# A hybrid Conformer/Mamba-2 block on one core: the order in which DVE issues the norm's multiplications and ACT the gate's sigmoids

## The chip, the core and the metric

The kernel runs on one core of a Trainium2 chip. A core has a matrix engine (TensorE, PE), a vector engine (VectorE, DVE), a scalar engine (ScalarE, ACT), a general engine (GpSimd, POOL) and a queue that starts transfers (SyncE, SP). Each works through its own list of instructions in order; semaphores make one wait for another. The metric is the device time of one launch in microseconds (us), the median of several runs.

## The reference

One layer over 1024 positions and 1024 channels in float32:

```python
u = h @ w_in[l]
u_glu, z, xbc, dt_raw, gate_a, gate_b = split_in(u)
y_a = conformer_branch(u_glu, ...)   # GLU, 31-tap depthwise conv, layer norm, SiLU, @ w_conv_out
y_b = ssd_branch(z, xbc, dt_raw, ...)
mix = (jax.nn.sigmoid(gate_a) * y_a + jax.nn.sigmoid(gate_b) * y_b) @ w_o[l]
h = layer_norm(DN_ALPHA * h + mix, ...)
ffn = conv_ffn(h, ...)
h = layer_norm(DN_ALPHA * h + ffn, ...)
```

The SSD branch ends, group by group (four groups of 512 channels), in a gated norm whose statistic is taken over the group's channels for each position:

```python
yg = (y * jax.nn.silu(z)).reshape(bsz, t, SSM_GROUPS, SSM_DIM // SSM_GROUPS)
yg = yg * lax.rsqrt(jnp.mean(jnp.square(yg), axis=-1, keepdims=True) + RMS_EPS)
yn = yg.reshape(bsz, t, SSM_DIM) * norm_w
return yn @ w_out
```

## The kernel before

Channels lie on the 128 partitions and positions run along the free axis. The 1024 positions are worked through in two halves of 512 (`hh` 0 and 1). Each half runs through `mixers`, `combine` and an output product; the FFN follows.

**Products.** Float32 accuracy comes from a split of both operands into a high and a low part, so that one step of a product is three matmuls (L170, L171, L172: high by high, high by low, low by high; only the third reads the low part of the weights). One product of `project` is eight such steps, 24 matmuls, into one of four PSUM banks of the pool `acc`. `weights` (L142) brings a 128x1024 block for each product: SyncE loads it (`st`, three buffers), ACT casts the high part (L147) and DVE subtracts for the low part (L151), into `w` (three buffers). In half 1 the low parts of most blocks are read back from memory instead.

**Mixers.** For each group g, PE makes the products for B, C and x, the gate z and two columns of the Conformer branch. DVE does the 4-tap convolutions (L408) and, as a filler of low priority, the 31-tap convolution, one tap of 128x512 an instruction (L453, c<-v). `ssd_group` then runs four chunks of 128 positions: ACT makes the decay matrix `m` (L504, L511), DVE multiplies it (L531), PE forms the chunk's output from it (L536, L539), and DVE adds the skip term to that output (L554, four instructions), gates it (L562) and, with ACT's squares (L564), sums up `ssum` (L565, L566). At the next group `scaled` turns `ssum` into the norm's row: PE sums over partitions (L573), ACT takes the root (L581), DVE the reciprocal (L582), POOL stores the row (L584) and loads it again spread over all partitions as `rstd` (L585), and DVE multiplies the group's four tiles by it (L588, 128x512 each). `parts` splits the product into `yT` (L601 on ACT, L602 on DVE), which the products with `w_ssm_out` read.

**Combine.** PE makes gate products (weights `w_gb_0` to `w_gb_7`) and SSD output products (`w_sp_0` to `w_sp_7`) in turn: gb_0, gb_1, sp_0, gb_2, sp_1, gb_3, sp_2 and so on. A sigmoid on ACT (L721) empties a gate's bank into `gb`. DVE adds an earlier half of the SSD output, loaded as `yb` (L730), into `mb` (L735) and multiplies it by `gb` (L736). POOL adds the convolution's channels (L681, L683) for its layer norm.

**What sets the order.** The kernel is written in the order of the algorithm; a scheduler with a model of time and with priorities decides the order in which each engine issues its instructions. Weights have a high priority (offset 4000), the 31-tap convolution a low one (−1500).

Of the kernel before, what the change touches and what calls it, by code (L numbers as in the profile page):

```python
# [8 lines left out]
F32 = mybir.dt.float32  # L9
F32R = mybir.dt.float32r  # L10
AF = mybir.ActivationFunctionType
ALU = mybir.AluOpType
# [43 lines left out]
def kernel(  # L56
# [42 lines left out]
    later = statep.tile([P, P], F32, name="later")  # L99
# [39 lines left out]
    }  # L139
    y_scr = [dram.tile([8, P, HALF], F32, name=f"y_scr{i}") for i in range(2)]  # L140

    def weights(src, name, keep=None, kept=None):  # L142
        with tc.high_priority(offset=4000):
            st = wst.tile([P, D], F32, tag="st", name=f"st_{name}")
            SY.dma_start(st, src)
            w = wsp.tile([P, 2, D], F32R, tag="w", name=f"w_{name}")
            A.copy(w[:, 0, :], st)  # L147
            if kept is not None:
                SY.dma_start(w[:, 1, :].bitcast(F32), kept)
            else:  # L150
                V.tensor_tensor(  # L151
                    out=w[:, 1, :], in0=st, in1=w[:, 0, :].bitcast(F32), op=ALU.subtract
                )
            if keep is not None:
                SY.dma_start(keep, w[:, 1, :].bitcast(F32))
        return w

    def col_weights(hh, ct):
        scr = low_scr.get(ct)
        return weights(  # L160
            wcol[ct], f"c{hh}_{ct}", None if hh else scr, scr if hh else None
        )

    def big_tile(name):
# [301 lines left out]
    def z_gate(pl, hh, hT, g):  # L466
# [3 lines left out]
            A.activation(out=zs[:, i, :], in_=column(hh, hT, CT_Z + 4 * g + i), func=AF.Silu)  # L470
        return zs

    def ssd_group(pl, hh, g, xT, BT, CT, zs):
        S = states[g]
        h8 = slice(8 * g, 8 * g + 8)
# [8 lines left out]
        for c in range(4):  # L484
            nm = f"{hh}_{g}_{c}"
            cs = slice(c * P, (c + 1) * P)
            first = hh == 0 and c == 0
            last = hh == 1 and c == 3
            ab = pl.tile([P, 8, P], F32, tag="ab", name=f"ab{nm}")
            r = c * HEADS + 8 * g  # L490
            SY.dma_start(
                ab.rearrange("p h l -> p (h l)"),
                acs_scr[hh][r : r + 8, :].rearrange("h l -> (h l)").partition_broadcast(P),
            )
            px = bank(0)
            for i in range(4):
                TE.transpose(px[:, i * P : (i + 1) * P], xT[:, i, cs], ident)
            pb = bank(0)
            if not last:
                TE.transpose(pb[:, :P], BT[:, cs], ident)  # L500
            TE.matmul(pb[:, P : 2 * P], BT[:, cs], CT[:, cs], start=True, stop=True)
            m = pl.tile([P, 8, P], F32, tag="m", name=f"m{nm}")
            for h in range(8):
                A.activation(  # L504
                    out=m[:, h, :],
                    in_=ab[:, h, :],
                    func=AF.Relu,
                    scale=-1.0,
                    bias=acs[:, c, 8 * g + h : 8 * g + h + 1],
                )  # L510
            A.activation(out=m, in_=m, func=AF.Exp, scale=-1.0)  # L511
            if not first:
                ce = pl.tile([P, 8, P], F32, tag="ce", name=f"ce{nm}")
                A.activation(out=ce, in_=ab, func=AF.Exp)  # L514
                G.tensor_tensor(  # L515
                    out=ce, in0=ce, in1=CT[:, cs].unsqueeze(1).to_broadcast([P, 8, P]), op=ALU.mult
                )
            cbm = pl.tile([P, P], F32, tag="cbm", name=f"cbm{nm}")
            V.tensor_mul(cbm, pb[:, P : 2 * P], upper)
            xs = pl.tile([P, HALF], F32, tag="xs", name=f"xs{nm}")  # L520
            V.tensor_tensor(
                out=heads(xs), in0=heads(px), in1=per_head(dts[0][:, c, h8]), op=ALU.mult
            )
            if not last:
                xsd = pl.tile([P, HALF], F32, tag="xsd", name=f"xsd{nm}")
                V.tensor_tensor(
                    out=heads(xsd), in0=heads(px), in1=per_head(dts[1][:, c, h8]), op=ALU.mult
                )
                bt = pl.tile([P, P], F32, tag="bt", name=f"bt{nm}")
                A.copy(bt, pb[:, :P])  # L530
            V.tensor_tensor(out=m, in0=m, in1=cbm.unsqueeze(1).to_broadcast([P, 8, P]), op=ALU.mult)  # L531
            py = bank(0)
            for i in range(4):
                pair = [(2 * i + k, py[k * HP : (k + 1) * HP, i * P : (i + 1) * P]) for k in (0, 1)]
                for h, o in pair:
                    TE.matmul(o, xs[:, h * HP : (h + 1) * HP], m[:, h, :], start=True, stop=first)  # L536
                if not first:
                    for h, o in pair:
                        TE.matmul(  # L539
                            o, S[:, h * HP : (h + 1) * HP], ce[:, h, :], start=False, stop=True  # L540
                        )
            if not last:
                pn = bank(0)
                TE.matmul(pn, bt, xsd, start=True, stop=True)
                if first:
                    V.tensor_copy(S, pn)
                else:
                    V.tensor_tensor(
                        out=heads(S), in0=heads(S), in1=per_head(edc[:, 1, c, h8]), op=ALU.mult
                    )  # L550
                    V.tensor_add(S, S, pn)
            for i in range(4):
                k = PC_SD + 4 * g + i
                V.scalar_tensor_tensor(  # L554
                    out=xT[:, i, cs],
                    in0=xT[:, i, cs],
                    scalar=pc[:, k : k + 1],
                    in1=py[:, i * P : (i + 1) * P],
                    op0=ALU.mult,
                    op1=ALU.add,  # L560
                )
            V.tensor_mul(xT[:, :, cs], xT[:, :, cs], zs[:, :, cs])  # L562
            sq = pl.tile([P, 4, P], F32, tag="sq", name=f"sq{nm}")
            A.activation(out=sq, in_=xT[:, :, cs], func=AF.Square)  # L564
            V.tensor_add(sq[:, 0:2], sq[:, 0:2], sq[:, 2:4])  # L565
            V.tensor_add(ssum[:, cs], sq[:, 0], sq[:, 1])  # L566

        def scaled():
            rstd = pl.tile([P, HALF], F32, tag="rstd", name=f"rstd{hh}_{g}")
            rows = pl.tile([P, P], F32, tag="rows", name=f"rows{hh}_{g}")  # L570
            pv = bank(0)
            for j in range(4):
                TE.matmul(  # L573
                    pv[j * HEADS : (j + 1) * HEADS, :P],
                    ones[:, :HEADS],
                    ssum[:, j * P : (j + 1) * P],
                    start=True,
                    stop=True,
                    tile_position=(0, j * HEADS),
                )  # L580
            A.activation(out=rows, in_=pv[:, :P], func=AF.Sqrt, bias=eps, scale=1.0 / HALF)  # L581
            V.reciprocal(out=rows, in_=rows)  # L582
            scr = nrm_scr[hh * GROUPS + g]
            G.dma_start(scr, rows.rearrange("(j r) l -> j r l", j=4)[:, 0, :])  # L584
            G.dma_start(rstd, scr.rearrange("j l -> (j l)").partition_broadcast(P))  # L585
            for i in range(4):
                k = PC_NW + 4 * g + i
                V.scalar_tensor_tensor(  # L588
                    out=xT[:, i, :],
                    in0=xT[:, i, :],  # L590
                    scalar=pc[:, k : k + 1],
                    in1=rstd,
                    op0=ALU.mult,
                    op1=ALU.mult,
                )

        def parts(yT):
            ks = slice((g % 2) * 4, (g % 2) * 4 + 4)
# [60 lines left out]
    def combine(hh, hT, yT, accs):  # L659

        with pool(f"comb{hh}") as pl:
            gbs = []
            squares = pl.tile([P, 2, HALF], F32, tag="sq", name=f"csq{hh}")
            stats = pl.tile([P, 2, HALF], F32, tag="stats", name=f"stats{hh}")
            late, cs = [], []
# [50 lines left out]
            def gate():  # L716
                j = len(gbs)
                pg = bank(1)
                project(pg, weights(wcol[CT_GB + j], f"gb{hh}_{j}"), hT)
                gb = pl.tile([P, HALF], F32, tag="gate", bufs=3, name=f"gb{hh}_{j}")  # L720
                A.activation(out=gb, in_=pg, func=AF.Sigmoid)  # L721
                gbs.append(gb)

            gate()
            mb = None
            for j in range(8):
                if j < 7:
# [4 lines left out]
                    mb = early_tiles()  # L732
                ps = bank(1)
                project(ps, weights(wssm[j, 1], f"sp{hh}_{j}"), yT)
                V.tensor_add(mb[j], ya, ps)  # L735
                V.tensor_mul(mb[j], mb[j], gbs[j])  # L736
                if j == 2 - hh:
# [567 lines left out]
```

## Time and profile before

| | |
|---|---|
| median of 3 runs | 1966.11 us (1964.66 to 1969.19) |
| profiled execution | 1962.23 us |
| its span | 1960.5 us |
| granted TensorE clock | 0.998 |
| instructions in the span | 25846 |

The profile is of one execution. A line of a timeline gives start and duration (us), engine, program line, operation, the tiles out<-in, and in brackets how long the engine stood still before it and what ended that. A line of waits gives the total, the number and the longest of the waits of one group. Half 0's combine begins at 484 us (PE's first matmul with `w_gb_0`), half 1's at 1127 us.

### The profile page before, as it was taken

Reading aid. Unit: us, or ns where it says so; the run is one execution under the profiler, and the core shown is the slowest. Engines: PE = TensorE matmul, PEld = TensorE weight load, DVE = VectorE, ACT = ScalarE, POOL = GpSimd, SP = SyncE. Lnnn points to the kernel's source line nnn. Section 1 sums busy time; section 2 is a strip of 40 time slices with the busy share of each in tenths; the row PEclk is TensorE's granted clock in tenths of the full one; section 3 lists DMA queues with packets and bytes.
Section 4 is the critical chain, followed back from the end, with each engine's and each line's share of the span. In section 5 each row is a group of like instructions: output and inputs, shape, how many; then the busy total and the mean of one; then the engine's idle time right before and its main releaser. Section 6 shows DMA issues by size and latency. Waiting matters only on the chain.

```text
span 1960.5 us, 25846 instructions
## 1 busy us (share of the span) xinstructions
PE 1928.3 (98%) x9453; PEld 1572.2 (80%) x9453; DVE 1599.4 (82%) x2224; ACT 1083.5 (55%) x1617; POOL 216.8 (11%) x258
## 2 busy tenths in 40 slices
PE   9999999999999999999999999999999999989997
PEld 7888777777788788888778888888888888868886
DVE  7599999999887548898999646587788888879778
ACT  4666667654263266868775435365555555544432
POOL 0001000111310000110201130001000000121010
PEclk9999999999999999999999999999999999999999
DMA  7645455556446665555554744566445455588673
GB/s 265 223 167 209 162 193 183 172 167 220 142 168 205 211 218 183 191 185 196 190 173 155 233 139 129 176 248 225 167 171 185 165 198 173 184 299 296 196 227 130
DMA packets 127648, 378.36 MB, mean 193 GB/s; under 512 B 15104, under 2 KB 15648, under 8 KB 127520
## 3 DMA queue, kind: packets, MB, share of 16 engines
q1 hardware_dynamic: 107424, 318.48, 48.2%
q0 software_dynamic: 13760, 46.69, 6.9%
q10 hardware_dynamic: 6336, 11.54, 1.6%
q8 instruction: 74, 1.21, 0.2%
q14 instruction: 54, 0.44, 0.1%
HBM read 289.99 MB, written 86.65 MB: 192 GB/s over the span
## 4 chain that ended last, share of the span: by engine, by line
PE 57%; DVE 10%; DMA 5%; ACT 2%; issue 2%; SPq 0%; DVEq 0%; ACTq 0%
PE acc L172 13%; PE acc L171 13%; PE acc L170 13%; PE sm L171 5%; PE sm L172 5%; PE sm L170 5%; DVE c L453 3%; DMA dr<-wdown 1%; DMA dr<-b_scr 1%; DVE w_dn L1093 1%; DMA b_scr<-fo 1%; DVE x L408 1%; PE sm L536 1%; DVE rows L231 1%; DVE rows L234 1%
## 5 line engine op out<-in xcount | busy, mean ns | idle before, releaser
L170 PE MATMUL acc<-hT,w_c 128*128 128x512 f32 x1000 | 391.9, 392 | 0.6 <-ACT x L406 0.6
L172 PE MATMUL acc<-hT,w_c 128*128 128x512 f32 x1000 | 390.2, 391 | 0.6 <-DVE w_c L151 0.5
L171 PE MATMUL acc<-hT,w_c 128*128 128x512 f32 x1000 | 390.6, 391 | 0.0
L453 DVE SCALAR_TENSOR_TENSOR c<-v,pc,c 128x512 f32<-128x512 f32 x480 | 372.2, 801 | 7.1 <-ACT c L442 4.6
L170 PEld LDWEIGHTS acc<-hT,w_c 128*128 128x128 f32 x1000 | 187.8, 188 | 41.6 <-issue 1.9
L172 PEld LDWEIGHTS acc<-hT,w_c 128*128 128x128 f32 x1000 | 187.7, 188 | 41.4 <-DVE w_c L151 1.7
L171 PEld LDWEIGHTS acc<-hT,w_c 128*128 128x128 f32 x1000 | 187.8, 188 | 39.5 <-issue 1.1
L147 ACT CAST w_c<-st_c 128x1024 fp32r<-128x1024 f32 x128 | 133.8, 1045 | 108.9 <-PE acc L172 82.3
L515 POOL TENSOR_TENSOR ce<-ce,xbc 128x1024 f32<-128x1024 f32 x28 | 80.1, 2861 | 678.6 <-ACT ce L514 678.6
L1092 ACT CAST w_dn<-dr 128x1024 fp32r<-128x1024 f32 (+1 forms) x73 | 68.8, 945 | 86.4 <-DMA dr<-wdown 32.8
L504 ACT ACTIVATE m<-ab,acs 128x128 f32<-128x128 f32 x256 | 78.4, 390 | 48.9 <-PE sm L536 47.7
L170 PE MATMUL sm<-h1s,w_s 128*128 128x512 f32 x264 | 102.7, 389 | 0.0
L171 PE MATMUL sm<-h1s,w_s 128*128 128x512 f32 x264 | 102.7, 389 | 0.0
L172 PE MATMUL sm<-h1s,w_s 128*128 128x512 f32 x264 | 102.2, 389 | 0.0
L151 DVE TENSOR_TENSOR w_c<-st_c,w_c 128x1024 fp32r<-128x1024 f32 x64 | 79.0, 1237 | 22.3 <-ACT w_c L147 22.1
L408 DVE SCALAR_TENSOR_TENSOR x<-u,pc,x 128x512 f32<-128x512 f32 x96 | 79.7, 842 | 4.0 <-ACT x L406 3.8
L1093 DVE TENSOR_TENSOR w_dn<-dr,w_dn 128x1024 fp32r<-128x1024 f32 (+1 forms) x73 | 78.6, 1086 | 4.0 <-ACT w_dn L1092 4.0
L172 PE MATMUL acc<-h1b,w_ue 128*128 128x512 f32 x176 | 68.8, 394 | 0.2 <-DVE w_ue L151 0.2
L170 PE MATMUL acc<-h1b,w_ue 128*128 128x512 f32 x176 | 68.6, 390 | 0.0
L171 PE MATMUL acc<-h1b,w_ue 128*128 128x512 f32 x176 | 68.5, 389 | 0.0
L170 PE MATMUL sm<-h1b,w_s 128*128 128x512 f32 x176 | 68.5, 389 | 0.0
L171 PE MATMUL sm<-h1b,w_s 128*128 128x512 f32 x176 | 68.5, 389 | 0.0
(325 smaller groups left out, 4533.9 us busy)
## 6 DMA issues: line engine op xcount, KB each, us to landing
st_c<-wcol SPq DMA_DIRECT2D x128, 512.0 KB, 4.4
low_scr<-w_c SPq DMA_DIRECT2D x64, 512.0 KB, 2.9
w_c<-low_scr SPq DMA_DIRECT2D x64, 512.0 KB, 4.4
ab<-acs_scr SPq DMA_DIRECT2D x32, 512.0 KB, 4.1
dr<-wdown SPq DMA_DIRECT2D x55, 256.0 KB, 5.3
st_wo<-wo SPq DMA_DIRECT2D x24, 512.0 KB, 4.1
st_ue<-wup SPq DMA_DIRECT2D x22, 512.0 KB, 3.9
first_scr<-first ACTq DMA_DIRECT2D x44, 256.0 KB, 3.0
```

The lines of the kernel that those rows point to most:

```text
L147: A.copy(w[:, 0, :], st)
L151: V.tensor_tensor(out=w[:, 1, :], in0=st, in1=w[:, 0, :].bitcast(F32), op=ALU.subtract)
L170: TE.matmul(ps, wa(0), xa(0), start=start, stop=False, skip_group_check=more)
L171: TE.matmul(ps, wa(0), xa(1), start=False, stop=False, skip_group_check=more)
L172: TE.matmul(ps, wa(1), xa(0), start=False, stop=stop, skip_group_check=more)
L231: V.scalar_tensor_tensor(out=t, in0=t, scalar=mv[:, i, 0:1], in1=g, op0=ALU.subtract, op1=ALU.mult)
L408: V.scalar_tensor_tensor(out=o, in0=u[:, k : k + HALF], scalar=pc[:, wc + k : wc + k + 1], in1=o, op0=ALU.mult, op1=ALU.add,)
L453: V.scalar_tensor_tensor(out=accs[i], in0=v[:, k : k + HALF], scalar=pc[:, wc + k : wc + k + 1], in1=accs[i], op0=ALU.mult, op1=ALU.add,)
L504: A.activation(out=m[:, h, :], in_=ab[:, h, :], func=AF.Relu, scale=-1.0, bias=acs[:, c, 8 * g + h : 8 * g + h + 1],)
L515: G.tensor_tensor(out=ce, in0=ce, in1=CT[:, cs].unsqueeze(1).to_broadcast([P, 8, P]), op=ALU.mult)
L1092: A.copy(w[:, 0, cs], src)
L1093: V.tensor_tensor(out=w[:, 1, cs], in0=src, in1=w[:, 0, cs].bitcast(F32), op=ALU.subtract)
```

## The change

`weights` keeps a list of the casts and of the low parts that it issues. A new helper, `issue_after`, tells the scheduler to issue one instruction after another one of the same engine; it adds an order and no semaphore.

- The four multiplications by the norm's row (`held`) of groups 0 to 2 are to be issued after the last of the four skip additions (L554) of the next group's chunk 0. Those of group 3 are to be issued after the low part of `w_gb_0`, the first weights of `combine`.
- Each gate's sigmoid is to be issued ahead of the fifth cast of weights after its own: ahead of `w_gb_3`'s cast for gb_0.

```diff
+    casts, los = [], []
...
-            A.copy(w[:, 0, :], st)
+            casts.append(A.copy(w[:, 0, :], st))
...
+                los.append(
+                    V.tensor_tensor(
+                        out=w[:, 1, :], in0=st, in1=w[:, 0, :].bitcast(F32), op=ALU.subtract
+                    )
                 )
...
+    def issue_after(later, earlier):
+
+        tc.add_manual_dep(
+            later.ins,
+            earlier.ins.name,
+            mybir.DependencyInfo(mybir.DependencyClass.NoSync, mybir.DependencyReason.DATA),
+            reason="issue order",
+        )
...
+    held = []
...
-                V.scalar_tensor_tensor(
+                skip = V.scalar_tensor_tensor(
                     out=xT[:, i, cs],
...
+            while held and c == 0:
+                issue_after(held.pop(), skip)
...
-                V.scalar_tensor_tensor(
+                by_row = V.scalar_tensor_tensor(
                     out=xT[:, i, :],
...
+                held.append(by_row)
...
-                A.activation(out=gb, in_=pg, func=AF.Sigmoid)
+                sigmoids.append((len(casts), A.activation(out=gb, in_=pg, func=AF.Sigmoid)))
                 gbs.append(gb)
 
             gate()
+            while held:
+                issue_after(held.pop(), los[-1])
...
                 project(ps, weights(wssm[j, 1], f"sp{hh}_{j}"), yT)
+                for n, sigmoid in sigmoids:
+                    if len(casts) > n + 4:
+                        issue_after(casts[n + 4], sigmoid)
+                sigmoids = [(n, i) for n, i in sigmoids if len(casts) <= n + 4]
```

The added lines shift the numbers: L151, L453, L554, L588, L602, L721 and L735 of before are L154, L466, L569, L605, L620, L739 and L759 after. What the scheduler then makes of it is seen in each engine's order of instructions.

DVE in half 0, group 1, from the tap ahead of the multiplications of group 0 (`x_0_0`) to the skip additions of group 1's chunk 0 (`x_0_1`) and the work on chunk 1 (`xs_1_1`). Before:

```order
L453 SCALAR_TENSOR_TENSOR c_1_1347<-v_1_1102,pc,c_1_1347 128x512
L588 SCALAR_TENSOR_TENSOR x_0_0_713<-x_0_0_713,pc,rstd_0_1919 128x512 x4
L408 SCALAR_TENSOR_TENSOR xbc_18_2274<-u_18_2273,pc,xbc_18_2274 128x512
L453 SCALAR_TENSOR_TENSOR c_2_2176<-v_2_1845,pc,c_2_2176 128x512
L151 TENSOR_TENSOR w_c_26_2408<-st_c_26_2406,w_c_26_2408 128x1024
L554 SCALAR_TENSOR_TENSOR x_0_1_1493<-x_0_1_1493,pc,sm_1969 128x128 x4
L408 SCALAR_TENSOR_TENSOR xbc_22_2315<-u_22_2314,pc,xbc_22_2315 128x512
L546 COPY state_106<-sm_1978 128x512
L521 TENSOR_TENSOR xs_1_1_2015<-sm_1992,dtv 128x512
```

And after:

```order
L466 SCALAR_TENSOR_TENSOR c_1_1347<-v_1_1102,pc,c_1_1347 128x512
L421 SCALAR_TENSOR_TENSOR xbc_18_2274<-u_18_2273,pc,xbc_18_2274 128x512
L466 SCALAR_TENSOR_TENSOR c_2_2176<-v_2_1845,pc,c_2_2176 128x512
L154 TENSOR_TENSOR w_c_26_2408<-st_c_26_2406,w_c_26_2408 128x1024
L421 SCALAR_TENSOR_TENSOR xbc_18_2274<-u_18_2273,pc,xbc_18_2274 128x512
L569 SCALAR_TENSOR_TENSOR x_0_1_1493<-x_0_1_1493,pc,sm_1969 128x128 x4
L605 SCALAR_TENSOR_TENSOR x_0_0_713<-x_0_0_713,pc,rstd_0_1919 128x512 x4
L421 SCALAR_TENSOR_TENSOR xbc_22_2315<-u_22_2314,pc,xbc_22_2315 128x512
L466 SCALAR_TENSOR_TENSOR c_2_2176<-v_2_1845,pc,c_2_2176 128x512
L561 COPY state_106<-sm_1978 128x512
L536 TENSOR_TENSOR xs_1_1_2015<-sm_1992,dtv 128x512
```

The multiplications moved from ahead of the skip additions to right behind them, and one more instruction of the 4-tap convolution stands ahead of both.

DVE in half 0's combine, from the low parts of `w_sp_1` on. Before:

```order
L151 TENSOR_TENSOR w_sp_1_4622<-st_sp_1_4620,w_sp_1_4622 128x1024
L453 SCALAR_TENSOR_TENSOR c_6_4222<-v_6_3506,pc,c_6_4222 128x512
L453 SCALAR_TENSOR_TENSOR c_7_4224<-v_7_3574,pc,c_7_4224 128x512 x3
L151 TENSOR_TENSOR w_gb_3_4654<-st_gb_3_4652,w_gb_3_4654 128x1024
L453 SCALAR_TENSOR_TENSOR c_7_4224<-v_7_3574,pc,c_7_4224 128x512 x5
L151 TENSOR_TENSOR w_sp_2_4688<-st_sp_2_4686,w_sp_2_4688 128x1024
L453 SCALAR_TENSOR_TENSOR c_7_4224<-v_7_3574,pc,c_7_4224 128x512 x2
L735 TENSOR_TENSOR mb_0_4528<-yb_0_4526,acc_4553 128x512
```

And after:

```order
L154 TENSOR_TENSOR w_sp_1_4622<-st_sp_1_4620,w_sp_1_4622 128x1024
L466 SCALAR_TENSOR_TENSOR c_6_4222<-v_6_3506,pc,c_6_4222 128x512
L466 SCALAR_TENSOR_TENSOR c_7_4224<-v_7_3574,pc,c_7_4224 128x512 x10
L154 TENSOR_TENSOR w_gb_3_4654<-st_gb_3_4652,w_gb_3_4654 128x1024
L759 TENSOR_TENSOR mb_0_4528<-yb_0_4526,acc_4553 128x512
L154 TENSOR_TENSOR w_sp_2_4688<-st_sp_2_4686,w_sp_2_4688 128x1024
L760 TENSOR_TENSOR mb_0_4528<-mb_0_4528,gb_0_4492 128x512
```

All the taps that are left stand ahead of `w_gb_3`'s low parts now, eleven where four stood, and the addition to `mb_0` stands ahead of `w_sp_2`'s low parts. Further up in the same list, `w_gb_0`'s low parts now stand two taps later than the last tap ahead of the multiplications before, and the multiplications right behind them. From the multiplications of group 3 to `w_gb_3`'s low parts there are 28 taps, where there were 23; from the second low part of `yT` on, 24, where there were 20.

ACT in half 0's combine, from the cast of `w_sp_1` on. Before:

```order
L147 CAST w_sp_1_4622<-st_sp_1_4620 128x1024
L147 CAST w_gb_3_4654<-st_gb_3_4652 128x1024
L147 CAST w_sp_2_4688<-st_sp_2_4686 128x1024
L721 ACTIVATE gb_0_4492<-acc_4462 128x512
L721 ACTIVATE gb_1_4524<-acc_4494 128x512
L721 ACTIVATE gb_2_4615<-acc_4585 128x512
```

And after:

```order
L149 CAST w_sp_1_4622<-st_sp_1_4620 128x1024
L739 ACTIVATE gb_0_4492<-acc_4462 128x512
L149 CAST w_gb_3_4654<-st_gb_3_4652 128x1024
L739 ACTIVATE gb_1_4524<-acc_4494 128x512
L149 CAST w_sp_2_4688<-st_sp_2_4686 128x1024
L739 ACTIVATE gb_2_4615<-acc_4585 128x512
```

The three sigmoids, which stood together behind the cast of `w_sp_2`, now stand one by one among the casts.

Elsewhere the lists shift with these: on SyncE the load of `yb_0` stands behind the load for `w_gb_4` and no longer behind those for `w_sp_3` and `w_gb_5`; on PE the chunks' outputs of half 0 stand up to three matmuls later, and in half 1 those of chunks 1 to 3 stand 6 to 9 matmuls later in groups 1 and 2 and 15 in group 3; POOL's order is as it was.

More of the change, by code (lines that the diff above doesn't have):

```diff
@@ L150, in weights @@
             else:
-                V.tensor_tensor(
-                    out=w[:, 1, :], in0=st, in1=w[:, 0, :].bitcast(F32), op=ALU.subtract
+                los.append(
+                    V.tensor_tensor(
+                        out=w[:, 1, :], in0=st, in1=w[:, 0, :].bitcast(F32), op=ALU.subtract
+                    )
                 )
@@ L661, in combine @@
         with pool(f"comb{hh}") as pl:
-            gbs = []
+            gbs, sigmoids = [], []
             squares = pl.tile([P, 2, HALF], F32, tag="sq", name=f"csq{hh}")
```

## The prediction

> **What bounds the kernel now.** I read the page's busy shares, then TensorE's (PE's) waits, then VectorE's (DVE's) waits, then the two places where they meet. The busy shares:
>
> ```profile
> PE 1928.3 (98%) x9453; PEld 1572.2 (80%) x9453; DVE 1599.4 (82%) x2224; ACT 1083.5 (55%) x1617; POOL 216.8 (11%) x258
> ```
>
> PE is idle for 1960.5 − 1928.3 = 32 us of its span, and no order of DVE or ACT can win more than that and the slow restarts behind it. What the change can touch are waits of PE on DVE and ACT inside the two halves' mixers and combines. From the waits of PE over the whole span (total us, times, longest us):
>
> ```profile
> PE sm L536 <- DVE m L531: 3.3, 3, 1.4
> PE acc L172 <- DVE w_gb L151: 1.8, 2, 1.4
> PE acc L170 <- ACT gb L721: 1.6, 1, 1.6
> PE acc L172 <- DVE w_sp L151: 0.9, 1, 0.9
> PE acc L170 <- ACT x L406: 0.6, 1, 0.6
> PE acc L172 <- DVE w_c L151: 0.5, 1, 0.5
> ```
>
> They sum to 8.7 us in nine stalls. One stall costs a little more than its idle time, as PE's timeline at the first gate product of half 0 shows (start, duration):
>
> ```profile
> 484.20 0.39 PE L170 MATMUL acc<-hT,w_gb 128*128 128x512 f32 x1
> 484.43 0.39 PE L171 MATMUL acc<-hT,w_gb 128*128 128x512 f32 x1
> 486.23 0.50 PE L172 MATMUL acc<-hT,w_gb 128*128 128x512 f32 x1 [1.41 <-DVE w_gb L151]
> 486.57 0.40 PE L170 MATMUL acc<-hT,w_gb 128*128 128x512 f32 x1
> ...
> 517.37 0.39 PE L172 MATMUL acc<-hT,w_gb 128*128 128x512 f32 x1
> ```
>
> The steady pitch is 0.23. Here 1.80 passes, 1.57 too much, and the next start is 0.11 late too: 1.68 for 1.41 of idle time, 0.27 more. So the nine stalls are worth 8.7 + 9 × 0.27 = 11.1 us: the ceiling of this change. By place: the mixers of half 0 hold m once (1.4), x (0.6) and w_c (0.5), with restarts 3.3; the combine of half 0 holds w_gb twice, gb and w_sp, 4.3 idle and 5.4 with restarts; the mixers of half 1 hold the other two m, 1.9 idle and 2.4 with restarts. The places of the m stalls:
>
> ```profile
> 445.01 0.44 PE L536 MATMUL sm<-m,xs 128*64 128x128 f32 x4 [1.41 <-DVE m L531]
> ...
> 943.79 0.44 PE L536 MATMUL sm<-m,xs 128*64 128x128 f32 x4 [0.82 <-DVE m L531]
> ...
> 1000.28 0.44 PE L536 MATMUL sm<-m,xs 128*64 128x128 f32 x4 [1.06 <-DVE m L531]
> ```
>
> Is DVE late there because it is full, or because it stood still earlier? The window of the mixers of half 0 (us, then busy PE, PEld, DVE, ACT, POOL, granted clock, DMA share, GB/s):
>
> ```profile
> 195.00:470.00 275.00, 270.73 (x1453) 215.68 (x1452) 267.68 (x399) 178.23 (x305) 25.76 (x14) 1.00 0.53 177
> ```
>
> DVE is 97% busy in it, idle for 7.3 us. DVE's waits at the norm's row, asked window by window (205:215, 300:312, 392:402 in half 0, then 845:858 in half 1):
>
> ```profile
> DVE x L588 <- DMA rstd<-nrm_scr: 4.0, 1, 4.0
> ...
> DVE x L588 <- DMA rstd<-nrm_scr: 1.0, 1, 1.0
> ...
> DVE x L588 <- DMA rstd<-nrm_scr: 2.3, 1, 2.3
> ...
> DVE x L588 <- DMA rstd<-nrm_scr: 1.3, 1, 1.3
> ```
>
> The first three sum to 7.3: all the idle time that DVE has in the mixers of half 0 is spent at the multiplications by a row that is still on its way.
>
> **The change, part by part.** Nothing is computed that was not, and no DMA is added. Three things move.
>
> *Multiplications behind chunk 0's outputs (mixers, groups 0 to 2).* DVE at the first of these places, and PE's output of chunk 0:
>
> ```profile
> 206.41 1.09 PE L536 MATMUL sm<-m,xs 128*64 128x128 f32 x16
> ...
> 210.34 2.74 DVE L588 SCALAR_TENSOR_TENSOR x<-x,pc,rstd 128x512 f32<-128x512 f32 x4 [4.03 <-DMA rstd<-nrm_scr]
> ...
> 215.46 1.12 DVE L554 SCALAR_TENSOR_TENSOR x<-x,pc,sm 128x128 f32<-128x128 f32 x4
> ```
>
> Without the wait (4.03) and the four (2.74 less an overlap of 0.1) DVE comes to L554 at about 208.8 if its row is the same, and 0.66 later with the one L408 that now stands ahead too: 209.5, when PE's output (206.41 + 1.09) is done, so it does not wait there. After 1.1 of L554 it comes to the multiplications at 210.6, and the row landed by 210.34. The wait is gone, not moved. That gives DVE 7.3 us in half 0. The m stall at 445.01 needs 1.41 of them, x and w_c 0.6 and 0.5. I take all three as gone: −3.3. Bounds: −1.7 (m alone, 1.41 + 0.27, ahead of which the 2.3 stand) and −3.3.
>
> *Group 3's multiplications behind the first gate's low parts, and the sigmoids (combine of half 0).* DVE's row there:
>
> ```profile
> 473.88 2.73 DVE L453 SCALAR_TENSOR_TENSOR c<-v,pc,c 128x512 f32<-128x512 f32 x4
> 480.97 2.74 DVE L588 SCALAR_TENSOR_TENSOR x<-x,pc,rstd 128x512 f32<-128x512 f32 x4 [4.36 <-DMA rstd<-nrm_scr]
> 483.63 1.41 DVE L453 SCALAR_TENSOR_TENSOR c<-v,pc,c 128x512 f32<-128x512 f32 x2
> 484.96 1.22 DVE L151 TENSOR_TENSOR w_gb<-st_gb,w_gb 128x1024 fp32r<-128x1024 f32 x1
> ...
> 490.82 5.17 DVE L453 SCALAR_TENSOR_TENSOR c<-v,pc,c 128x512 f32<-128x512 f32 x3
> ...
> 513.19 1.22 DVE L151 TENSOR_TENSOR w_gb<-st_gb,w_gb 128x1024 fp32r<-128x1024 f32 x1
> ```
>
> and ACT's:
>
> ```profile
> 473.52 1.06 ACT L147 CAST w_gb<-st_gb 128x1024 fp32r<-128x1024 f32 x1 [2.47 <-PE acc L172]
> ...
> 503.60 1.05 ACT L147 CAST w_gb<-st_gb 128x1024 fp32r<-128x1024 f32 x1 [5.57 <-PE acc L172]
> ...
> 510.69 1.57 ACT L721 ACTIVATE gb<-acc 128x512 f32<-128x512 f32 x3
> ```
>
> The first gate's high parts are cast by 474.6, so its low parts can follow two more convolution taps (1.33 from 483.63 to 484.96, so 0.66 each) at about 478: the stall of 1.41 goes. The first sigmoid now stands ahead of the cast at 503.60, where before the three came two casts later, so the bank that PE waited 1.6 for is free by 503: gone too. But in the new order 28 taps, not 23, stand between the multiplications and w_gb_3's low parts (the eleven in a row among them), and one low part fewer: 5 × 0.66 − 1.14 = +2.16. Those low parts, which began at 513.19, begin at 515.35 and end at 516.6, if the multiplications still start with the row at 480.97. PE used them at 517.37, after 5.4 of stalls; without stalls it is there at 512.0. So a new stall stands at this product, and the combine's gain is 517.4 − 516.7 = 0.7 plus whatever lead DVE brings to 480.97. The lead is at most 7.3 − 3.3 = 4.0, and at least 0; the reciprocal and the row's two DMAs follow DVE's row, so a lead moves the row too. I take the middle, 2.0: −2.7, with bounds −0.7 and −4.7.
>
> In half 1 the same edit moves the four, which end as yT's low parts begin, to behind w_gb_0's low parts:
>
> ```profile
> 1114.82 2.43 DVE L602 TENSOR_TENSOR yT<-x,yT 128x1024 fp32r<-128x1024 f32 x2
> 1118.40 1.23 DVE L151 TENSOR_TENSOR w_gb<-st_gb,w_gb 128x1024 fp32r<-128x1024 f32 x1 [1.15 <-ACT w_gb L147]
> ...
> 1138.08 0.39 PE L170 MATMUL acc<-yT,w_sp 128*128 128x512 f32 x1
> ```
>
> They run from 1119.6 to 1122.3, where they ended at 1114.8, and yT's low parts end at 1124.7. PE wants yT at 1138.08: 13 us of cover, cost nothing. If that cover were gone, each us would be one of PE's.
>
> *PE's chunk outputs, which follow DVE's new row.* In half 1 the outputs of chunks 1 to 3 move 6 to 15 matmuls later. The stall at 1000.28 belongs to group 2's chunk 3, now 6 matmuls later, 6 × 0.23 = 1.4 > 1.06: gone, −1.3. That at 943.79 is a chunk 0 and stays in place; whether DVE's 1.3 from 845 lasts until there is open. I take half of its 1.1: together −1.8, bounds 0 and −2.4.
>
> [...] In the row at 490.82 three taps take 5.17 us instead of 3 × 0.66: POOL's adds of the convolution's means (9.3 us, next fence) run there. Over the nine taps of the rows at 490.82 and 498.14 the excess is 5.17 + 5.09 − 9 × 0.66 = 4.3.
>
> ```profile
> 489.97 2.09 POOL L681 TENSOR_TENSOR stats<-cc 128x512 f32<-128x512 f32 x1
> 492.14 7.23 POOL L683 TENSOR_TENSOR stats<-stats,cc 128x512 f32<-128x512 f32 x4
> ...
> 498.14 5.09 DVE L453 SCALAR_TENSOR_TENSOR c<-v,pc,c 128x512 f32<-128x512 f32 x6
> ```
>
> These 4.3 are in the times that I moved. Were DVE stopped for all 9.3, its row would be 5.0 later, which is rival A. [...]
>
> *Sum.* −3.3 − 2.7 − 1.8 = −7.8 us. The profiled execution took 1962.23 (span 1960.5 and 1.7 around it), so 1954.4 on its terms; it is 3.9 below the median of 1966.11, so the forecast for the median is 1958.3. A measurement of this kernel can tell about 0.2%, 3.9 us, from no change.
>
> **The rivals.**
> A. *The new wait at w_gb_3 is the larger one.* POOL's adds fall wholly on DVE's row: low parts 5.0 later, and the combine loses 2.3 instead of gaining 2.7. Total −3.3 + 2.3 − 1.8 = −2.8: 1963.3. For: 24 taps now stand between yT's and w_gb_3's low parts, 20 before. Against: 4.3 of 9.3 so far.
> B. *The time at L588 was not what made PE late.* DVE gives the recovered time back at other waits, or the scheduler's row puts another wait in its place; the PE stalls stay or move. For: no stall of PE names L588. Against: 97% busy, and the idle 7.3 are all there. Then only the sigmoid's stall is touched, 0 to −3: 1964.6, the same.
> C. *Slower: DVE stands at mb_0.* In half 0 the addition to mb_0 moves from behind w_sp_2's low parts to ahead of them, and needs yb_0:
>
> ```profile
> 519.84 6.19 SPq L730 DMA_DIRECT2D yb<-y_scr  x4
> ...
> 523.60 0.69 DVE L735 TENSOR_TENSOR mb<-yb,acc 128x512 f32<-128x512 f32 x1 [2.79 <-DMA yb<-y_scr]
> ```
>
> From SyncE's issue to w_sp_2's low parts pass 3.8 + 0.7 + 1.2 = 5.7; PE wants them at 522.8 on the clock of before. SyncE's row now has yb_0 behind w_gb_4's load, two loads earlier, which speaks against. If its tile came free only later, the issue at 519.84 would cost 2.7 there, and each us later one more, with w_gb_4 and w_sp_3 queued behind it on DVE. It decides the sign from an issue at 517.1 + 5.1 (the gains elsewhere) = 522.2; at 527 it gives +4.8: 1970.9.
>
> **How the numbers follow.** Forecast 0.60 (gain of 4 to 11, all faster); A 0.15 (a third of it a gain over 3.9); B 0.16 (nearly all same); C 0.09 (slower). Faster 0.60 + 0.05 = 0.65; same 0.10 + 0.15 = 0.25; slower 0.09 + 0.01 = 0.10. The range reaches down to all 11.1 gone and one us of stalls too short to be listed, 1966.1 − 12.1 = 1954.0, and up to 1966.5, which leaves out C and a little of B.
>
> **What would show it.** Right: no wait on rstd of over 0.5 us at groups 0 to 2 of either half; no PE wait on gb's sigmoid; PE's waits on m and w_c gone in half 0; one wait of 1 to 4 us on w_gb at the fourth gate product, and none at the first. Wrong: PE's waits on m stay in half 0 although the waits on rstd are gone (B); a wait on w_sp at its third product with DVE standing at yb (C); DVE waiting at L554 instead of L588, or a granted clock under 1.00 in these windows.

## The result and the profile after

The change takes 1961.73 us (median of 10 runs, 1959.13 to 1963.09) against 1965.18 us for the kernel before (10 runs): a ratio of 0.9978, 95% interval 0.9969 to 0.9987. It is faster by 0.2%, a little under half of what was forecast, and inside the range. The profiled execution took 1960.26 us, its span is 1958.4 us.

PE's busy share and its waits on DVE, POOL and ACT, from the page and from the waits of the whole span:

```profile
PE 1929.1 (99%) x9453; PEld 1574.9 (80%) x9453; DVE 1599.8 (82%) x2224; ACT 1081.2 (55%) x1615; POOL 218.9 (11%) x258
```

```profile
PE acc L185 <- DVE w_gb L154: 4.2, 1, 4.2
...
PE sm L551 <- DVE m L546: 2.7, 2, 2.5
```

The seven stalls that were counted in half 0 are gone, and two larger ones stand in the list: one of 4.2 us on `w_gb` in half 0's combine, and one of 2.5 on `m` in half 1. (L551, L546, L185 and L154 are L536, L531, L172 and L151 of before.) The window of half 0's mixers, in the columns used before:

```profile
195.00:470.00 275.00, 274.96 (x1478) 220.66 (x1477) 271.94 (x410) 182.99 (x310) 28.83 (x22) 1.00 0.54 184
```

PE is idle for 0.04 us in it, where it was idle for 4.3, and DVE has 4.3 us more of work done in the same time. At the first of the moved places DVE's timeline reads:

```profile
208.41 1.14 DVE L569 SCALAR_TENSOR_TENSOR x<-x,pc,sm 128x128 f32<-128x128 f32 x4
209.53 2.74 DVE L605 SCALAR_TENSOR_TENSOR x<-x,pc,rstd 128x512 f32<-128x512 f32 x4
```

No bracket stands behind either: neither PE's output nor the norm's row is waited for. The only wait for the row that the list of the whole span still has is the one of group 3 in half 0, behind the low parts of `w_gb_0`, where 4.36 us were waited before:

```profile
DVE x L605 <- DMA rstd<-nrm_scr: 1.8, 1, 1.8
...
472.73 2.74 DVE L605 SCALAR_TENSOR_TENSOR x<-x,pc,rstd 128x512 f32<-128x512 f32 x4 [1.77 <-DMA rstd<-nrm_scr]
```

Then the combine of half 0. PE at the first and at the fourth gate product:

```profile
477.63 0.39 PE L183 MATMUL acc<-hT,w_gb 128*128 128x512 f32 x1
...
505.06 0.39 PE L184 MATMUL acc<-hT,w_gb 128*128 128x512 f32 x1
509.67 0.80 PE L185 MATMUL acc<-hT,w_gb 128*128 128x512 f32 x1 [4.22 <-DVE w_gb L154]
510.26 0.63 PE L183 MATMUL acc<-hT,w_gb 128*128 128x512 f32 x1
510.69 0.63 PE L184 MATMUL acc<-hT,w_gb 128*128 128x512 f32 x1
```

From 477.63 to 505.06 PE does not stop once. It then stands still for 4.6 us from start to start, and the matmuls behind that come at a pitch of 0.43 us, not 0.23. DVE at that place:

```profile
497.94 1.22 DVE L154 TENSOR_TENSOR w_sp<-st_sp,w_sp 128x1024 fp32r<-128x1024 f32 x1
499.07 9.41 DVE L466 SCALAR_TENSOR_TENSOR c<-v,pc,c 128x512 f32<-128x512 f32 x11
508.39 1.22 DVE L154 TENSOR_TENSOR w_gb<-st_gb,w_gb 128x1024 fp32r<-128x1024 f32 x1
```

The eleven taps run without a low part between them, 9.41 us, and ACT had the high parts ready 13 us earlier:

```profile
494.15 1.06 ACT L149 CAST w_gb<-st_gb 128x1024 fp32r<-128x1024 f32 x1 [3.89 <-PE acc L185]
```

The windows around the stall show the slow matmuls as a granted clock (the third figure from the end):

```profile
500.00:510.00 10.00, 5.78 (x26) 4.50 (x25) 9.68 (x12) 2.18 (x3) 3.01 (x2) 0.89 0.31 105
510.00:520.00 10.00, 10.00 (x35) 8.04 (x35) 6.08 (x7) 1.54 (x2) 0.74 (x1) 0.77 0.64 211
```

By stages, from PE's starts in the two traces (first output of the first chunk; first matmul with `w_gb_0`; first with the convolution's weights; the same two in half 1; first with the FFN's weights up, then down; last matmul), in us:

| stretch of PE | before | after | difference |
|---|---|---|---|
| up to the first output | 113.55 | 112.62 | −0.93 |
| mixers of half 0 | 370.65 | 365.01 | −5.64 |
| gate and SSD products of half 0 | 94.31 | 95.65 | +1.34 |
| to half 1's combine | 548.69 | 549.95 | +1.26 |
| gate and SSD products of half 1 | 88.80 | 88.80 | 0 |
| to the FFN's first product | 93.60 | 93.29 | −0.31 |
| FFN up | 417.21 | 417.28 | +0.07 |
| FFN down | 220.44 | 222.69 | +2.25 |

The first row and the last lie outside of what the change moves; the last is between 220.3 and 224.3 in the traces of the experiments below, whatever their kernel. The mixers gave 5.6 us; the combine of half 0 and the mixers of half 1 took 2.6 of them back.

### The profile page after: what moved, and what is told of

Read it like the earlier page. It is cut to its first block, busy times and chain, and to the rows that moved or that the text cites. A ratio compares the mean times of both kernels' runs of the same rounds, so it can differ in the third digit from the quotient of the medians.

```text
span 1958.4 us, 25837 instructions
## 1 busy us (share of the span) xinstructions
PE 1929.1 (99%) x9453; PEld 1574.9 (80%) x9453; DVE 1599.8 (82%) x2224; ACT 1081.2 (55%) x1615; POOL 218.9 (11%) x258
## 4 chain that ended last, share of the span: by engine, by line
PE 60%; DVE 10%; DMA 3%; ACT 2%; issue 2%; DVEq 0%; SPq 0%; ACTq 0%
PE acc L185 13%; PE acc L184 13%; PE acc L183 13%; PE sm L184 6%; PE sm L185 6%; PE sm L183 6%; DVE c L466 4%; DMA dr<-wdown 1%; DVE x L421 1%; DMA st_wo<-wo 1%; DMA b_scr<-fo 1%; PE sm L551 1%; PE sm L554 0%; DVE m L546 0%; ACT m L519 0%
## 5 line engine op out<-in xcount | busy, mean ns | idle before, releaser
L185 PE MATMUL acc<-hT,w_c 128*128 128x512 f32 x1000 | 391.1, 391 | 0.0
L466 DVE SCALAR_TENSOR_TENSOR c<-v,pc,c 128x512 f32<-128x512 f32 x480 | 369.7, 798 | 7.3 <-ACT c L455 4.5
L185 PEld LDWEIGHTS acc<-hT,w_c 128*128 128x128 f32 x1000 | 187.8, 188 | 40.0 <-issue 1.5
L185 PE MATMUL sm<-h1s,w_s 128*128 128x512 f32 x264 | 102.2, 389 | 0.0
L154 DVE TENSOR_TENSOR w_c<-st_c,w_c 128x1024 fp32r<-128x1024 f32 x64 | 79.4, 1243 | 22.3 <-ACT w_c L149 17.1
L185 PE MATMUL acc<-h1b,w_ue 128*128 128x512 f32 x176 | 68.8, 394 | 0.3 <-DVE w_ue L154 0.3
## 6 DMA issues: line engine op xcount, KB each, us to landing
st_c<-wcol SPq DMA_DIRECT2D x128, 512.0 KB, 4.4
low_scr<-w_c SPq DMA_DIRECT2D x64, 512.0 KB, 2.9
w_c<-low_scr SPq DMA_DIRECT2D x64, 512.0 KB, 4.4
ab<-acs_scr SPq DMA_DIRECT2D x32, 512.0 KB, 4.1
st_wo<-wo SPq DMA_DIRECT2D x24, 512.0 KB, 4.5
st_ue<-wup SPq DMA_DIRECT2D x22, 512.0 KB, 3.6
```

The costliest lines, as they stand in the source:

```text
L154: V.tensor_tensor(out=w[:, 1, :], in0=st, in1=w[:, 0, :].bitcast(F32), op=ALU.subtract)
L185: TE.matmul(ps, wa(1), xa(0), start=False, stop=stop, skip_group_check=more)
L466: V.scalar_tensor_tensor(out=accs[i], in0=v[:, k : k + HALF], scalar=pc[:, wc + k : wc + k + 1], in1=accs[i], op0=ALU.mult, op1=ALU.add,)
```

## The experiments

Theory 1: the multiplications' new place frees DVE of its waits, and PE of its stalls, up to `w_gb_3`; there the sigmoids' new place draws in seven more taps and makes one stall that eats more than the combine had to give. Theory 2, the rival, says that DVE is simply full, or that the time won is given back wherever it is won. Each kernel was compared with the kernel before on the same chip. Three chips were used, on which the kernel before took 1965.85 us (the first four experiments), 1964.64 us (the instructions on a tile of their own) and 1964.15 us (the other four). The ratios are uncertain by some 0.1%, so the medians of two experiments, on two chips above all, can be told apart to 2 or 3 us only. What is smaller is read from PE's stretches in the traces, each of which is one execution.

**The sigmoids one cast later.** Each sigmoid goes ahead of the sixth cast after its own:

```diff
-                    if len(casts) > n + 4:
-                        issue_after(casts[n + 4], sigmoid)
-                sigmoids = [(n, i) for n, i in sigmoids if len(casts) <= n + 4]
+                    if len(casts) > n + 5:
+                        issue_after(casts[n + 5], sigmoid)
+                sigmoids = [(n, i) for n, i in sigmoids if len(casts) <= n + 5]
```

> The whole change, but each sigmoid is ordered ahead of the sixth cast of weights after its own (that of w_sp_2 for gb_0) and no longer the fifth (w_gb_3), which leaves four taps, not eleven, ahead of w_gb_3's low parts. Theory 1 (the change wins about 11 us of PE's time before w_gb_3 and gives 7 of it back at one new stall, which comes from the eleven taps that the sigmoid's place draws in): the stall of 4.2 us on w_gb and the slow matmuls behind it are gone, the bank is free in time since the sigmoid runs at about 495 and PE wants it at 499, and a wait of at most 1 us at w_sp_2's low parts (now behind seven taps) takes their place; the median is 5 to 7 us below the change's 1961.7, at 1955 to 1957. Theory 2 (DVE is full in this stretch, whatever the order): the lateness moves to w_sp_2 with 3 us or more and the median stays within 2 us of the change's.

Measured: 1955.8 us, ratio 0.9944 (0.9931 to 0.9957). PE has no wait at all between 195 and 600 us; its gate and SSD products take 88.90 us, against 94.31 before and 95.65 in the change. DVE and ACT there:

```profile
499.00 3.90 DVE L466 SCALAR_TENSOR_TENSOR c<-v,pc,c 128x512 f32<-128x512 f32 x4
502.82 1.22 DVE L154 TENSOR_TENSOR w_gb<-st_gb,w_gb 128x1024 fp32r<-128x1024 f32 x1
503.95 5.47 DVE L466 SCALAR_TENSOR_TENSOR c<-v,pc,c 128x512 f32<-128x512 f32 x7
509.34 1.22 DVE L154 TENSOR_TENSOR w_sp<-st_sp,w_sp 128x1024 fp32r<-128x1024 f32 x1
```

```profile
494.07 1.06 ACT L149 CAST w_gb<-st_gb 128x1024 fp32r<-128x1024 f32 x1 [4.38 <-PE acc L185]
495.03 0.59 ACT L739 ACTIVATE gb<-acc 128x512 f32<-128x512 f32 x1
```

The sigmoid runs at 495.03, right behind the cast of `w_gb_3`, and PE takes the bank at 499.31: ahead of that cast or behind it, the bank is free in time. All that the place ahead of the cast did was to put eleven taps where four stand here. Theory 1 holds: the lateness did not move on to `w_sp_2`.

**The sigmoids alone.** Without the order of the multiplications:

```diff
-            while held and c == 0:
-                issue_after(held.pop(), skip)
...
-            while held:
-                issue_after(held.pop(), los[-1])
```

> Only the sigmoids' order; the multiplications by the norm's row stay where they were. Theory 1: the mixers are as before; the wait of 1.6 us for the bank goes, but eleven taps in place of four stand ahead of w_gb_3's low parts, 7 x 0.78 = 5.5 us later at about 519.8, where PE without the bank's wait comes at 515.6: a stall of about 4 us on w_gb, and the clock halved behind it for 2.6 us as in the change. Half 0's combine loses 4 to 5 us on before, and the median is 2 to 5 us above before's, 1967 to 1970. Theory 2: the sigmoids' order is a gain of its own, 1.8 us: 1963.4.

Measured: 1968.62 us, ratio 1.0017 (1.0007 to 1.0026): slower by 0.2%, as theory 1 had it. PE's waits in half 0:

```profile
PE acc L185 <- DVE w_gb L154: 6.2, 2, 4.4
```

The longer of the two is `w_gb_3`, 4.4 us. The other is `w_gb_0`, 1.85 us, and half-speed matmuls follow both; behind the longer the granted clock is 0.85 (from 520 to 530). The combine takes 99.15 us, 4.8 more than before. So the part of the change that was to free a bank is a loss by itself.

**The multiplications alone**, the other half of the change:

```diff
-                for n, sigmoid in sigmoids:
-                    if len(casts) > n + 4:
-                        issue_after(casts[n + 4], sigmoid)
-                sigmoids = [(n, i) for n, i in sigmoids if len(casts) <= n + 4]
```

> Only the multiplications' order (all four groups); the sigmoids stay where they were. Theory 1: mixers of half 0 as in the change (5.7 us), the first stall on w_gb (1.7 with its restart) gone, the wait for the bank at the second SSD output product still there (1.9 with its restart), no stall of over 1.5 us at w_gb_3; half 1 as in the change. Median 6 to 8 us below before's, 1957 to 1959. Theory 2: as the change, 1961 to 1963.

Measured: 1957.83 us, ratio 0.9959 (0.9948 to 0.9971). The one wait of PE between 195 and 600 us is that for the bank:

```profile
PE acc L183 <- ACT gb L739: 1.6, 1, 1.6
```

**The multiplications of groups 0 to 2 alone**, with group 3's where they were:

```diff
-            while held:
-                issue_after(held.pop(), los[-1])
...
-                held.append(by_row)
+                if g < 3:
+                    held.append(by_row)
```

and no order of the sigmoids.

> Only the multiplications of groups 0 to 2, in the mixers; group 3's stay ahead of w_gb_0's low parts. Theory 1: mixers of half 0 as in the change, 5.7 us ahead when w_gb_0's product begins; there the wait on w_gb_0 is as before (1.4) or shorter by DVE's lead; the other waits of the combine as before. Median 5 to 6 us below before's, 1959 to 1960. Theory 2 (time won in the mixers is given back at once): within 2 us of before, 1963 to 1967.

Measured: 1959.14 us, ratio 0.9964 (0.9952 to 0.9976). The mixers take 364.91 us, as in the change. The combine's waits:

```profile
PE acc L183 <- ACT gb L740: 1.6, 1, 1.6
PE acc L185 <- DVE w_sp L154: 0.9, 1, 0.9
PE acc L185 <- DVE w_gb L154: 0.4, 1, 0.4
```

DVE's lead over PE from the mixers, about 1 us here, takes the first `w_gb` stall from 1.4 to 0.4; the rest is as before.

**Half 1 left as it was**, in the version with the sixth cast:

```diff
-                held.append(by_row)
+                if not hh:
+                    held.append(by_row)
```

> The version with the sigmoids ahead of the sixth cast, with the multiplications' order given in half 0 only; in half 1 they stand as before. Theory 1 (in half 1 the new place of the multiplications makes group 2's last chunk later, so that PE's stall on m there grows from 1.1 to 2.5 us, with a slow clock behind it in some executions): that stall is 1.1 again, that of group 2's first chunk (0.8) comes back, PE's way from half 1's mixers to its combine is 0.8 to 2.5 us shorter; the median is 0 to 2 us below the 1955.8 of the version with both halves, 1953.8 to 1955.8. Theory 2 (the stall grows only because PE comes earlier): it stays at 2.5 and the median does not fall.

Measured: 1955.01 us, ratio 0.9955 (0.9943 to 0.9967). Its time cannot be told from the version with both halves (0.9944), but its trace can: the way to half 1's combine takes 548.67 us, as before (548.69), where the change took 549.95 and the version with both halves 551.56 (in that execution the slow clock followed the stall; in the change's, where the granted clock is 1.00 from 985 to 1010, it did not). PE's waits on `m` in half 1 are the old ones:

```profile
PE sm L551 <- DVE m L546: 1.9, 2, 1.1
```

So the growth of that stall comes from the multiplications' place in half 1, and not from PE's earlier arrival. It is one of the two quickest versions that ran.

**DVE's time put back.** In the version with the sixth cast, eleven instructions, 6, 2 and 3 a group, which change no value:

```diff
+            if not hh and g < 3:
+                for n in range((6, 2, 3)[g]):
+                    held.append(
+                        V.scalar_tensor_tensor(
+                            out=xT[:, n % 4, :],
+                            in0=xT[:, n % 4, :],
+                            scalar=ones[:, 0:1],
+                            in1=xT[:, n % 4, :],
+                            op0=ALU.mult,
+                            op1=ALU.max,
+                        )
+                    )
```

> The version with the sigmoids ahead of the sixth cast, with eleven instructions of DVE added behind the multiplications of half 0's groups 0 to 2 (6, 2 and 3, each x*1 max x on 128x512, so no value changes): 11 x 0.66 = 7.3 us, as much as DVE's waits for the row took before. Theory 1 (PE's gain in the mixers is the DVE time that the waits gave free): PE's first gate product in half 0 starts 3 to 6 us later than in the version without them (477.6), PE's waits on DVE in the mixers are back, and the median is 1959 to 1962. Theory 2 (the gain is from PE's new order of chunk outputs, and DVE had time to spare): start and median within 1.5 us of it, 1955 to 1957.

Measured: 1967.46 us, ratio 1.0017 (1.0009 to 1.0026), and the first gate product starts at 485.77. That is 8.2 us later, more than theory 1 allowed, and the reason is not the one meant: one wait, on ACT, with the slow clock behind it (a matmul every 0.43 us).

```profile
238.00 0.80 PE L183 MATMUL acc<-hT,w_c 128*128 128x512 f32 x1 [4.87 <-ACT x L419]
```

The added instructions lie on the way to `yT`, so that ACT's casts of `yT` wait for them too, and ACT's order changed with them: the instruction that empties PE's bank (L419) began at 237.28, behind the work on the decay matrix, where the version without them had it at 221.91. So the run changes more than DVE's time. As a test of DVE's time it is inconclusive, so it was run again with the instructions on a tile of their own:

```diff
+                            out=spare, in0=spare, scalar=ones[:, 0:1], in1=spare,
...
+                    issue_after(held[-1], by_row)
```

> As the run that put DVE's time back, but the eleven added instructions work on a tile of their own (spare*1 max spare, 128x512), ordered behind the multiplications of half 0's groups 0 to 2, so that neither yT nor ACT waits for them; only DVE's 7.3 us are taken. The taps, which fill DVE's free time, are pushed back: 16 instead of 7 now stand between the low parts of w_gb_3 and w_sp_2. Theory 1 (PE's gain is the DVE time that the waits gave free): waits of PE on DVE come back, some in the mixers and one of 3 to 6 us on w_sp_2's low parts, and the median is 4 to 8 us above the 1955.8 of the version without them, 1960 to 1964. Theory 2 (the gain is from PE's order of chunk outputs alone): within 2 us of it.

Measured: 1964.02 us, ratio 0.9996 (0.9986 to 1.0006), 8 us above the version without them (10 by the two ratios), just past the range given. The mixers keep their gain (the first gate product starts at 477.8) and the bill comes in the combine:

```profile
PE acc L187 <- DVE w_sp L156: 6.7, 1, 6.7
```

DVE's 7.3 us stand there as 6.7 us of PE's. The taps give way in the mixers and are all late in the end. Theory 1 holds for half 0 as a whole, where DVE had no time to spare; the waits that it expected back in the mixers did not come, so there the gain does not hang on DVE's free time.

**The stall on `w_gb_3` by length.** In the version with the sixth cast, two instructions, and then three, between cast and low parts:

```diff
             casts.append(A.copy(w[:, 0, :], st))
+            if name == "gb0_3":
+                for _ in range(2):
+                    V.scalar_tensor_tensor(
+                        out=st, in0=st, scalar=ones[:, 0:1], in1=st, op0=ALU.mult, op1=ALU.max
+                    )
```

> The version with the sigmoids ahead of the sixth cast, with two DVE instructions of 1.2 us added between the cast and the low parts of half 0's w_gb_3 (st*1 max st, no value changes). The low parts come at about 508.0, PE wants them at 505.2: a stall of 2.8 us. Theory 1 (a stall costs its length, and a slow clock of 2 to 3 us more follows only when it is long, over about 3 us): span up by 3, 1958 to 1959, no slow matmuls behind it. Theory 2 (any such stall is followed by half-speed matmuls): up by 5.5, 1961.

Measured: 1959.92 us, ratio 0.9975 (0.9966 to 0.9985). The stall is 2.0 us, not 2.8, and no slow matmul follows it; the gate and SSD products take 91.05 us, 2.15 more than without. The median does not decide between the theories: it is 4.1 above that of the version without, or 5.8 with each taken against the kernel before on its chip. The trace, which is for theory 1, is one execution. No run shows a limit at theory 1's 3 us: in the run with the sigmoids alone half-speed matmuls followed a stall of 1.85 us, and in the version with the sixth cast the 2.5 us on `m` in half 1.

```profile
PE acc L190 <- DVE w_gb L159: 2.0, 1, 2.0
```

> As the run before with three such instructions: low parts at about 509.9, a stall of 4.7 us as in the change. Both theories: half-speed matmuls behind it, 4 to 5 us of them, costing 2.6; median 7 above the version without, 1962 to 1964. If no slow matmuls follow, the slow clock in the change was not from the length of the stall.

Measured: 1960.54 us, ratio 0.9982 (0.9973 to 0.999), 4.7 above the version without, or 6.4 with each taken against the kernel before on its chip; 7 was expected.

```profile
PE acc L190 <- DVE w_gb L159: 4.3, 1, 4.3
```

The stall is that of the change, 4.3 us, and half-speed matmuls follow it, but five at a pitch of 0.43 us where the change had ten: the products take 94.81 us, 5.9 more than without, of which 4.45 are the stall and 1.5 the clock. The trace's record of the granted clock has one stretch at half speed here, 3.41 us long, of which 3.0 lie behind the stall; in the change it is 6.83 us long, and 5.0 lie behind it. Half of these is what the clock cost, 1.5 and 2.5. That half-speed matmuls follow is as expected; the price of the slow clock is smaller here, 1.5 us where 2.6 was expected.

## Why the prediction was right, and where it was not

The direction and the range held, and so did the mechanism of the mixers; the size did not: 3.5 us between the medians, 7.8 forecast. The gain is nearer to rival A's 2.8 than to the forecast, but not by A's way, so that nearness is luck. Two steps of the sum failed: nothing was put down for a slow clock behind the new stall, and half 1 was to gain.

- **Mixers of half 0: −3.3 forecast, −5.64 measured.** The waits for the norm's row are gone and not moved, as said, and so are all the stalls counted, about 3.7 us with their restarts. Of the other 2.0, 1.6 are a row that the prediction left out of its ceiling: PE's two waits on `ssum`, taken to cost nothing. From before's timeline:

```profile
285.48 0.55 PE L497 MATMUL sm<-ident,x 128*128 128x128 f32 x3
286.82 0.41 PE L573 MATMUL sm<-ssum,ones 128*32 128x128 f32 x2 [0.80 <-DVE ssum L566]
```

  The step between these two kinds of matmul took 1.07 and 1.19 us; after the change it takes 0.31. That PE's outputs stand up to three matmuls later, 0.7 us, does not explain the gain by itself. At the place of the old `m` stall, before and after:

```profile
443.66 1.21 DVE L531 TENSOR_TENSOR m<-m,cbm 128x1024 f32<-128x1024 f32 x1
445.01 0.44 PE L536 MATMUL sm<-m,xs 128*64 128x128 f32 x4 [1.41 <-DVE m L531]
...
435.42 1.22 DVE L546 TENSOR_TENSOR m<-m,cbm 128x1024 f32<-128x1024 f32 x1
438.45 0.44 PE L551 MATMUL sm<-m,xs 128*64 128x128 f32 x4
```

  `m` was done 0.14 us ahead of PE, and is done 1.81 us ahead of it now: more than the 0.7 us, so DVE itself is earlier.

- **Combine of half 0: −2.7 forecast, +1.34 measured.** All four old stalls went, 5.5 us, by the steps given, and the new stall came at the product named. It was sized at 2.7 and is 4.4 start to start, but not because the low parts came late. On before's times (the trace after is 0.93 us ahead from PE's first output on), the low parts of `w_gb_3` were forecast to end at 516.6 − 3.3 − 2.0 = 511.3 and ended at 510.5; PE was forecast there at 512.0 − 3.3 = 508.7 and was there at 506.2. What PE had gained more in the mixers it waited off here. So up to the end of this stall the two stages gained 6.8 us, and 6.0 were forecast. What failed is the term that comes behind it and that the sum did not have: the slow clock, 2.5 us.
- **Why the low parts were not earlier still.** The lead guessed at 2.0 was good: the multiplications of group 3 began 8.24 us earlier than before, PE's first gate product 6.57, a lead of 1.7. From there to the low parts of `w_gb_3` DVE took 35.7 us and not 32.2 + 2.16 = 34.4. The last eleven taps took 9.41 us where 11 × 0.66 is 7.3: from one tap on `c_7` to the next it is 0.79 us eight times, and 1.69 once, beside an addition of POOL's. Only that last 1.0 us is lost beside POOL, as rival A has it. No run shows DVE stopped for the whole of POOL's additions, as A's 5.0 us supposed: in the trace of before four taps took 1.77 us each instead of 0.74, 1.0 more, beside additions of 1.6 to 2.15 us. A's weighing in the prediction was itself off. Beside POOL's additions a low part lost time too (the first line; the next one takes 1.22), which adds 1.1 to the 4.3 counted; and an addition takes 1.29 us with DVE standing still (the second line), up to 2.15 beside DVE, so that the 9.3 us hold time that POOL lost as well:

```profile
495.91 2.31 DVE L151 TENSOR_TENSOR w_sp<-st_sp,w_sp 128x1024 fp32r<-128x1024 f32 x1
...
520.95 1.29 POOL L683 TENSOR_TENSOR stats<-stats,c 128x512 f32<-128x512 f32 x1 [9.02 <-DVE c L453]
```

- **Half 1: −1.8 forecast, +1.26 measured.** This is the larger miss, 3.1 us. The stall of group 2's first chunk went. That of its last chunk was to go, because PE's output moved 6 matmuls later; it grew instead:

```profile
997.14 0.44 PE L551 MATMUL sm<-m,xs 128*64 128x128 f32 x4 [2.52 <-DVE m L546]
...
995.77 1.23 DVE L546 TENSOR_TENSOR m<-m,cbm 128x1024 f32<-128x1024 f32 x1 [0.97 <-ACT m L526]
...
994.68 1.06 ACT L526 ACTIVATE m<-m 128x1024 f32<-128x1024 f32 x1
```

  DVE's `m` waited 0.97 us for ACT's exponential, which began at 994.68. ACT had waited until 985.08 for DVE's 4-tap convolution and then worked without a break up to that exponential, 9.6 us, where 8.8 passed before. The prediction looked at PE's and DVE's order there and not at ACT's. That the multiplications' place is the cause is shown by the run that left half 1 alone; through which instruction of ACT or DVE was not tried. PE's waits on `m` in half 1 grew by 0.8 us in all; where the other 0.5 of the 1.26 come from was not traced.
- **Half 1's combine: nothing forecast, nothing measured** (88.80 both times): the 13 us of cover held.
- **Rival B** is ruled out: the time at the row was what made PE late, and the multiplications alone keep 8 us. **Rival C** did not come about: the addition to `mb_0` ran at 509.53 without a wait for `yb`.
- **The signs.** Of those for being right all came but one, the wait on `w_gb`, which is 4.2 us where 1 to 4 was given. One of those for being wrong came too, a granted clock under 1.00 in these windows: 0.89 and 0.77.
- **Why eleven taps.** A sigmoid ordered ahead of a cast puts that cast's low parts behind the sigmoid too. In the change these are the low parts of `w_gb_3`, and they stand right behind the last tap; with the sixth cast those of `w_sp_2` stand there. Why the scheduler waits for the last tap is open. That it cannot place the combine's tiles before the mixers' are given up would explain it; this was only argued.

## What to carry to other kernels

Where a full engine waits for a transfer at one instruction, move that instruction behind the next thing that it must wait for anyway. Here DVE's waits for the row in half 0 fell from 11.7 us to 1.8, and the multiplications alone took 8.0 us off the median. An order given on one engine changes the order on the others: read the place that you name in every engine's list, and give the latest order that still serves (here the sixth cast, not the fifth). Size a new stall with the durations of the instructions as they will stand, with what runs beside them, and add what can come behind it (here 2.5 us of slow clock).

## What the runs showed of the hardware

A stall was paid for twice. Behind the stall of 4.4 us ten of PE's matmuls came at 0.43 us instead of 0.23. In the eleven traces of this case (from 20 to 1895 us of the span, gaps from start to start of two matmuls), all 5 gaps of over 4.6 us were followed by such matmuls, 5 of 8 gaps of 2.9 us, and 8 of 69 of 1.2 to 2.6 us, each slow stretch put down to the last gap ahead of it. The record of the granted clock has 18 stretches at half speed there, and each is 3.41 or 6.83 us long (12 and 6). The same place of the same length, half 1's stall of 2.9 us, had one in some executions and not in others. Four single gaps of 1.75 to 2.24 us are among those that were followed by it; in the trace of before two of 2.02 us were not. So the length of the gap alone does not tell whether it follows, and what decides it was not shown.
